# Sparse attention as four strands beside dense products, score tiles in accumulator banks, and a tile's wide products in a run

## The chip, the core and the metric

The kernel runs on one NeuronCore of a Trainium2 chip. TensorE (PE) multiplies into eight PSUM banks, VectorE (DVE) and ScalarE (ACT) empty those banks and do the elementwise work, GpSimd (POOL) does a little elementwise work in SBUF, and SyncE (SP) issues the loads. The metric is the device time of one execution in microseconds. Before the change the median of three runs is 1178.96 us (1177.51 to 1179.39).

## What is computed

Two transformer layers over 256 tokens of width 1024, everything in float32:

```python
for layer in range(DEPTH):                       # DEPTH = 2
    h = layer_norm(ALPHA * h + 0.5 * swiglu(h, ffn_w_in[layer, 0], ffn_w_out[layer, 0]), ...)
    mix = hybrid_mixer(h, ...) if layer % 2 == 0 else nsa_mixer(h, positions, ...)
    h = layer_norm(ALPHA * h + mix, ...)
    h = layer_norm(ALPHA * h + 0.5 * swiglu(h, ffn_w_in[layer, 1], ffn_w_out[layer, 1]), ...)

def swiglu(x, w_in, w_out):                      # inner width 2816
    gate, up = jnp.split(x @ w_in, 2, axis=-1)
    return (jax.nn.silu(gate) * up) @ w_out
```

So there are four feed-forward stages, one hybrid stage and one sparse attention stage (`nsa_mixer`). Sparse attention has 16 query heads in 2 groups of 8; a group shares its keys and values. For each block of 128 queries it adds three attentions, each weighted by a gate: over 15 compressed key blocks (a small two-layer network over 32 tokens each), over the selected blocks, and over a window. With 256 tokens there are four selectable blocks of 64 and up to eight may be taken, so the selected attention is causal attention over all keys, and the window of 512 also covers all of them. Both use keys turned by a partial rotary embedding. The sum over heads goes through an output product.

## The kernel before

Every product is made from float32 numbers that are split in two float32r parts, hi and lo: hi by hi, hi by lo and lo by hi are added up in one PSUM bank. `split` copies hi (ACT or DVE) and subtracts it (DVE) for lo. Weights arrive in `raw` tiles of 1 MB, of which there are three, and every weight part is split on the chip into `whi` and `wlo` tiles: one ACT or DVE copy, and one DVE subtraction (`wlo<-raw,whi`) each.

Nothing is issued as it is written. The class `Plan` records all operations of the program, and `Plan.order` lays them out with a list scheduler: each engine takes the ready operation that can start first, and among equals the one recorded earliest; its prices and buffer rules decide the order on each engine. On the chip every engine then runs its list strictly in that order. Within the stages the recording order is set by `weave`: it takes turns among generators (strands), each with a weight, so that the strand with the least PE work per weight is next; a strand that yields `'wait'` is passed over.

PSUM is dealt out by tag: `ps` has 2 banks, `mp` 2, `acc` 4. `ps` serves projections, `mp` transposes and small products, `acc` the sums of output products.

**Feed-forward stages.** Most inner features are made with weights as the stationary side: `proj_two` makes one tile of 128 features for all 256 tokens. Its stationary weights `whi` meet x's hi and lo parts side by side (one matmul of 512 columns), and `wlo` meets x's hi part (256 columns). Over the eight slices of the width it records them in turn, 512, 256, 512, 256. Each step of 256 features loads one `raw` tile for the gate and one for the up half and calls `proj_two` four times.

**The sparse attention stage** (`nsa`). `b` is the block of 128 queries or tokens (0 or 1), `g` the head group. `kv(b)` makes keys, values and gates of block b, `queries(g, w, bs)` makes queries (two transposes through `mp`, with the rotary turn between them), `keys(b)` turns the keys and splits them into `kd` hi and lo. `compress()` makes the compressed keys and values, `cmp_probs(b)` their probabilities, `attend(g, b)` the two other attentions with all of the output of a group and block, and `out_g0` the part of the output product that needs only group 0. In `attend` a score tile fills one bank: two heads of 128 keys for block 0, one head of 256 keys for block 1, each twice (selected and window). DVE takes the row maxima out of the bank (`TENSOR_REDUCE`), ACT the exponentials (`P`), then the tile is scaled (`P<-P,arena`, 128x1024, DVE or POOL), transposed through `mp` and copied (`PT`), and multiplied with the values (`vtok`).

Before the change these lines set the order of that stage:

```python
for b in range(2):
    kv(b)
    for _ in queries(0, wq, [b]):
        pass
    keys(b)
...
SB, turn = (("ps", "ps", "acc"), ("ps",)), [0]
...
self.weave([(attention(), W_NSA[0]), (rest(), W_NSA[1]), (out_g0(), W_NSA[2])])
```

So all keys and all queries of group 0 come first, then three strands: attention; `rest`, which is the first part of `compress`, the queries of group 1, the second part of `compress` and `cmp_probs`; and `out_g0`.

Of the kernel before, what the change touches and what calls it, by code (L numbers as in the profile page):

```python
# [13 lines left out]
OP = mybir.AluOpType  # L14
# [4 lines left out]
P = 128  # L19
# [20 lines left out]
NSA_ORDER = 1  # L40
W_HYB, W_OUT, W_NSA = (90.0, 94.0), (15.0, 21.0), (55.0, 45.0, 20.0)
# [477 lines left out]
class K:  # L519
# [201 lines left out]
    def proj_tok(self, x, b, w, ps):  # L721

        mm = self.nc.tensor.matmul
        for k in range(KD):
            xh, xl = self.xb(x, b, k)
            mm(ps, xh, w[k][0], start=k == 0, stop=False)
            mm(ps, xl, w[k][0], start=False, stop=False)
        for k in range(KD):
            mm(ps, self.xb(x, b, k)[0], w[k][1], start=False, stop=k == KD - 1)

# [734 lines left out]
    def nsa(self, x, then):  # L1465
# [6 lines left out]

        def chunk(r):
# [14 lines left out]
        def kv(b):  # L1488
            for r in range(2):
                ps = self.bank("ps")  # L1490
                self.proj_tok(x, b, ws[r], ps[:, :280])
# [3 lines left out]
        self.rope_tables()  # L1495
# [34 lines left out]
        def queries(g, w, bs):  # L1530
            gs = slice(g * 512, (g + 1) * 512)
            for b in bs:
# [17 lines left out]
                for e, (hi, lo) in enumerate(((up, dn), (dn, up))):  # L1550
                    src = H3(pt, 4)[hi]
                    self.copy(s[hi, :, e, :], src)
                    V.tensor_tensor(s[lo, :, e, :], src, s[hi, :, e, :].bitcast(F32), OP.subtract)
        kd = [self.m4(1024, f"kd{n}", dtype=F32R).rearrange("p (g r t) -> p g r t", g=2, r=2) for n in range(2)]
# [24 lines left out]
        state = dict(q=False, c=False, o=-1)  # L1579

        def compress():
            F = self.m4(1024, "F").rearrange("p (v g t) -> p v g t", v=2, g=2)
            pr = self.sm([32, P], "pr")
            with self.late():
                nc.sync.dma_start(pr, i['nsa_cmp_pos'][0].rearrange("v (i two) d -> (v i) (two d)", two=2))
            pt = self.bank("mp")
            nc.tensor.transpose(pt[:, :32], pr, self.ident[:32, :32])
            pos = self.sm([P, 2, 16], "cpos")
            V.tensor_copy(pos, H3(pt[:, :32], 2))
            w2r = self.sm([P, 2, 2, 64], "w2r")  # L1590
            with self.late():
                nc.sync.dma_start(w2r, i['nsa_cmp_w2'][0].rearrange("v (a p) d -> p v a d", p=P))
            w2d = self.sm([P, 2, 2, 64], "w2d")
            for c in range(2):
                nc.gpsimd.tensor_copy(w2d[:, :, c, :], w2r[:, 0])
            w = self.unit_cols(w_in, 1024, 256)
            X = self.m4(1024, "X").rearrange("p (v k g c) -> p v k g c", v=2, k=16, g=2)
            nc.gpsimd.memset(X[:, :, :, :, 15:16], 0.0)
            for v in range(2):
                ps = self.bank("ps")[:, :T]  # L1600
                yield from self.proj_steps(x, w[v], ps)
# [8 lines left out]
            yield 'mid'  # L1610
# [43 lines left out]
        def cmp_probs(b):  # L1654
# [19 lines left out]
            V.tensor_tensor(ev, ev, mx[:, 2, :, None].to_broadcast([P, 16, 15]), OP.mult)  # L1674
            yield
# [3 lines left out]
            self.copy(eT[b], H3(pt[:, :256], 2))  # L1679

# [6 lines left out]
        SB, turn = (("ps", "ps", "acc"), ("ps",)), [0]  # L1687

        def attend(g, b):
            N = (b + 1) * P  # L1690
            per = 2 - b
            gv = gat[:, b, :].rearrange("p (h r) -> p r h", r=3)
            PT = {}
            for half in range(2):
                sc = self.sm([P, 2, 2, 4], "asum", bufs=4)
                tiles = []
                for h0 in range(0, 4, per):
                    ps = self.bank(SB[g][turn[0] % len(SB[g])])
# [6 lines left out]
                    for n in range(per):  # L1705
                        h = half * 4 + h0 + n
# [18 lines left out]
                hs = g * 8 + half * 4  # L1725
# [170 lines left out]
```

## Time and profile before

| | |
|---|---|
| median of 3 runs | 1178.96 us |
| the profiled execution | 1176.69 us |
| its span, first to last instruction | 1175.0 us |
| mean granted TensorE clock | 0.98 of 2.4 GHz |
| PE, DVE, ACT, POOL busy | 1139.2, 897.6, 499.8, 47.9 us |
| sparse attention stage | 827.3 to 981.7 us of the span |

The profile comes from one execution. A line of the page or of an answer names engine, operation, the tile written, the tiles read, shapes and the number of instructions. PE's busy time counts matmuls whose ends are modelled and overlap, so the time from one matmul's start to the next one's is the better measure of its cost. The granted clock is 1.00 at 2.4 GHz and 0.50 at 1.2 GHz.

### The profile page before, as it was taken

How to read it: one execution, taken by the hardware profiler on the slowest of the kernel's cores; microseconds unless marked ns; L12 is line 12 of the kernel's file. 1: busy time of each engine (PE TensorE's matmuls, PEld its weight loads, DVE VectorE, ACT ScalarE, POOL GpSimd, SP SyncE). 2: the span in 40 equal slices, each digit the busy share in tenths (PEclk: the TensorE clock that was granted, in tenths of full speed). 3: DMA queues.
4: the chain of work that ended last, by engine and by line, in shares of the span. 5: the costliest groups of instructions: out<-in, count | busy, mean ns of one | idle time of the engine just before them, and what ended most of it. 6: DMA issues, size and time to landing. Idle time of an engine off the chain costs nothing.

```text
span 1175.0 us, 16522 instructions
## 1 busy us (share of the span) xinstructions
PE 1139.2 (97%) x6572; PEld 961.5 (82%) x6572; DVE 897.6 (76%) x1494; ACT 499.8 (43%) x911; POOL 47.9 (4%) x75
## 2 busy tenths in 40 slices
PE   8999999998999999999999999999998889999997
PEld 6888888898899777888888888888976667888886
DVE  7977778789699889777768967775867778777755
ACT  5534332367334555533333633333446345433320
POOL 1000000001021000000000000000002000000000
PEclk9999999999999999999999999999988799999999
DMA  8866553542305346755563756545236326755520
GB/s 298 310 188 200 194 201 90 161 155 95 108 30 188 121 164 217 251 181 179 193 203 119 272 180 204 186 150 183 86 99 147 105 72 215 251 198 180 192 75 36
DMA packets 144166, 196.14 MB, mean 167 GB/s; under 512 B 9277, under 2 KB 121050, under 8 KB 144090
## 3 DMA queue, kind: packets, MB, share of 16 engines
q1 hardware_dynamic: 144090, 195.10, 50.4%
q8 instruction: 51, 0.84, 0.3%
q14 instruction: 25, 0.20, 0.1%
HBM read 194.04 MB, written 1.05 MB: 166 GB/s over the span
## 4 chain that ended last, share of the span: by engine, by line
PE 88%; DVE 6%; DMA 2%; ACT 2%; issue 1%; SPq 0%; DVEq 0%; ACTq 0%
PE ps L495 53%; PE acc L495 29%; PE mp L495 6%; DVE wlo L495 2%; DMA raw<-in_ffn_w_in_dram 1%; DVE h L495 1%; DVE arena L495 1%; DMA raw<-in_nsa_w_out_dram 1%; DMA arena<-in_nsa_cmp_pos_dram 0%; SPq L495 0%; DVE x L495 0%; DVE cv L495 0%; ACT sw L495 0%; DVE lnst L495 0%; ACT P L495 0%
## 5 line engine op out<-in xcount | busy, mean ns | idle before, releaser
L495 PE MATMUL ps<-x,whi 128*128 128x512 f32 (+2 forms) x1680 | 516.9, 367 | 8.4 <-DVE cv L495 4.9
L495 DVE TENSOR_TENSOR wlo<-raw,whi 128x1024 fp32r<-128x1024 f32 (+1 forms) x349 | 415.7, 1212 | 9.8 <-ACT whi L495 6.5
L495 PE MATMUL ps<-x,wlo 128*128 128x256 f32 (+1 forms) x1432 | 404.7, 283 | 0.0
L495 PEld LDWEIGHTS ps<-x,whi 128*128 128x128 f32 (+1 forms) x1680 | 302.3, 190 | 64.4 <-issue 6.9
L495 PEld LDWEIGHTS ps<-x,wlo 128*128 128x128 f32 (+1 forms) x1432 | 272.1, 190 | 2.9
L495 ACT ACTIVATE whi<-raw 128x1024 fp32r<-128x1024 f32 (+1 forms) x243 | 245.5, 1049 | 24.9 <-DMA raw<-in_ffn_w_in_dram 17.0
L495 PE MATMUL acc<-whi,g 128*128 128x512 f32 x704 | 230.9, 391 | 0.0
L495 ACT ACTIVATE sg<-ps 128x256 f32<-128x256 f32 x162 | 62.2, 384 | 351.6 <-PE ps L495 351.4
L495 DVE TENSOR_TENSOR sg<-ps,sg 128x256 f32<-128x256 f32 x162 | 68.7, 424 | 165.1 <-ACT sg L495 165.0
L495 PEld LDWEIGHTS acc<-whi,g 128*128 128x128 f32 x704 | 132.2, 188 | 29.4
L495 PE MATMUL acc<-wlo,g 128*128 128x512 f32 x352 | 137.8, 392 | 0.0
L495 PE MATMUL ps<-whi,x 128*128 128x512 f32 (+1 forms) x480 | 126.5, 389 | 3.3 <-DVE whi L495 2.4
L495 PEld LDWEIGHTS ps<-whi,x 128*128 128x128 f32 x480 | 86.3, 190 | 23.0 <-DVE whi L495 3.7
L495 PEld LDWEIGHTS acc<-wlo,g 128*128 128x128 f32 x352 | 66.1, 188 | 10.9
L495 DVE CAST whi<-raw 128x1024 fp32r<-128x1024 f32 (+2 forms) x106 | 71.7, 678 | 4.1 <-DMA raw<-in_ffn_w_in_dram 2.9
L495 PE MATMUL ps<-wlo,x 128*128 128x512 f32 (+1 forms) x240 | 67.7, 382 | 0.0
L495 PE MATMUL acc<-whi,x 128*128 128x512 f32 x192 | 67.0, 413 | 0.1
L495 PEld LDWEIGHTS ps<-wlo,x 128*128 128x128 f32 x240 | 43.4, 189 | 7.7
L495 ACT ACTIVATE sg<-sg 128x256 f32<-128x256 f32 x74 | 31.1, 421 | 38.1 <-DVE sg L495 38.1
L495 POOL TENSOR_TENSOR lnve<-lnve,mhalf 128x1 f32<-128x1 f32 x12 | 11.4, 953 | 797.8 <-DVE lnve L495 797.8
L495 PEld LDWEIGHTS acc<-whi,x 128*128 128x128 f32 x192 | 35.7, 189 | 9.8 <-issue 2.8
L495 DVE SCALAR_TENSOR_TENSOR cv<-ps,arena,cv 128x255 f32<-128x255 f32 (+2 forms) x84 | 39.9, 477 | 4.8 <-ACT cv L495 3.8
(245 smaller groups left out, 971.9 us busy)
## 6 DMA issues: line engine op xcount, KB each, us to landing
raw<-in_ffn_w_in_dram SPq DMA_DIRECT2D x74, 1024.0 KB, 5.0
raw<-in_ffn_w_out_dram SPq DMA_DIRECT2D x44, 1024.0 KB, 5.0
raw<-in_hyb_w_in_dram SPq DMA_DIRECT2D x22, 1024.0 KB, 5.0
raw<-in_ffn_w_in_dram SPq DMA_DIRECT2D x26, 512.0 KB, 4.0
raw<-in_hyb_w_out_dram SPq DMA_DIRECT2D x8, 1024.0 KB, 4.8
raw<-in_nsa_w_in_dram SPq DMA_DIRECT2D x5, 1024.0 KB, 5.1
raw<-in_nsa_cmp_w_dram SPq DMA_DIRECT2D x4, 1024.0 KB, 5.7
raw<-in_nsa_w_out_dram SPq DMA_DIRECT2D x8, 512.0 KB, 7.7
```

The costliest lines, as they stand in the source:

```text
L495: r = getattr(getattr(nc, eng), fn)(*[res(a) for a in args], **{k: res(a) for k, a in kw.items()})
```

## The change

It has three parts.

1. `proj_two` records a tile's eight products of 512 columns first, and then its eight of 256.
2. The sparse attention stage is recorded as four strands with the weights 70, 55, 30 and 10: `attention`, `dense`, `compressed`, `out_g0`. `dense` is keys and values of block 0, queries of group 0 and block 0, keys and values of block 1, the first part of the compression (`compress_in`), queries of group 0 and block 1, and the queries of group 1. So attention of block 0 is recorded beside the products of block 1. Strands wait for what they need by names in a set `done`. The gate's sigmoid is done for each block by itself. The position table and the small second weights of the compression, and the tables of the rotary turn, are loaded and made at the stage's beginning.
3. Score tiles take their banks by `NSA_SB`: group 0, block 0 in `acc` alone, group 0, block 1 in `acc` and `ps` in turn, group 1 in `ps` alone. A tile's heads are now every other head of a group and not four neighbours, so the weights of the output product are loaded in plain rows: four loads of 1 MB on 128 partitions, where there were eight of 512 KB on 64 partitions.

```diff
-NSA_ORDER = 1
-W_HYB, W_OUT, W_NSA = (90.0, 94.0), (15.0, 21.0), (55.0, 45.0, 20.0)
+NSA_SB = (("acc",), ("acc", "ps"), ("ps",), ("ps",))
+W_HYB, W_OUT, W_NSA = (90.0, 94.0), (15.0, 21.0), (70.0, 55.0, 30.0, 10.0)
...
         for k in range(KD):
             mm(ps, w[0][:, k, :], x[2][:, k].rearrange("p h b t -> p (h b t)"), start=k == 0, stop=False)
+        for k in range(KD):
             mm(ps[:, :T], w[1][:, k, :], self.xk(x, k)[0], start=False, stop=k == KD - 1)
...
-        for b in range(2):
-            kv(b)
-            for _ in queries(0, wq, [b]):
-                pass
-            keys(b)
-        self.sigmoid(gat, gat)
-        for b in range(2):
-            self.scale_h(b)
+        def dense():
+            for b in range(2):
+                yield from kv(b)
+                if b == 1:
+                    yield from compress_in()
+                yield from queries(0, wq, [b])
+                keys(b)
+                self.sigmoid(gat[:, b], gat[:, b])
+                done.add(("k", b))
+                self.scale_h(b)
+                yield
+            yield from queries(1, self.tok_weights(w_in, 512, 512), range(2))
...
-                    ps = self.bank(SB[g][turn[0] % len(SB[g])])
+                    ps = self.bank(SB[2 * g + b][turn[0] % len(SB[2 * g + b])])
...
-                        h = half * 4 + h0 + n
+                        h = 2 * (h0 + n) + half
...
+                    yield from wait(("k", b), ("q", g, b))
                     yield from attend(g, b)
-                state['o'] = g
+                    done.add(("o", g, b))
-        def rest():
-            cmp = compress()
-            for r in cmp:
-                if r == 'mid' and NSA_ORDER:
-                    break
-                yield
-            yield from queries(1, self.tok_weights(w_in, 512, 512), range(2))
-            state['q'] = True
-            yield from cmp
+        def compressed():
+            yield from compress()
             for b in range(2):
+                yield from wait(("q", 0, b), ("q", 1, b))
                 yield from cmp_probs(b)
-            state['c'] = True
...
-            srcs = [(lambda r, s=s: v3(r)[HALF[s]], w_out[g, s, :, j0:j0 + 2, :]) for s in range(2)]
-            parts = self.unit(srcs, [lambda r, e=e: v3(r)[:, e, :] for e in range(2)])
+            parts = self.unit_rows(w_out, 2 * t, 2, 0, D)
...
-        self.weave([(attention(), W_NSA[0]), (rest(), W_NSA[1]), (out_g0(), W_NSA[2])])
+        self.weave(list(zip((attention(), dense(), compressed(), out_g0()), W_NSA)))
```

What this does to the engines' lists shows at three places. The first is PE in the last feed-forward stage, where `ps` is a tile of `proj_two`, `x` the stage's input and `sg` an earlier tile that is transposed. Before:

```order
L495 MATMUL ps_9152<-x_8884,whi_8924 128x512
L495 MATMUL ps_9152<-x_8884,wlo_8938 128x256
L495 MATMUL ps_9152<-x_8884,whi_8924 128x512
L495 MATMUL mp_9167<-ident_116,sg_9154 128x128 x2
L495 MATMUL ps_9152<-x_8884,wlo_8938 128x256
```

And after, the same tile and the next:

```order
L496 MATMUL ps_9151<-x_8895,whi_8911 128x512 x7
L496 MATMUL mp_9164<-ident_116,sg_9153 128x128 x2
L496 MATMUL ps_9151<-x_8895,whi_8911 128x512
L496 MATMUL ps_9151<-x_8895,wlo_8960 128x256 x8
L496 MATMUL ps_9184<-x_8895,whi_8950 128x512 x8
L496 MATMUL ps_9184<-x_8895,wlo_8992 128x256 x8
```

Wide and narrow products, which took turns, now stand in two runs of eight; the number of matmuls on PE is the same in the whole program (6097).

The second place is PE at the first scores. `whi` and `wlo` at 128x512 make queries, at 128x280 keys and values, `fixed` adds the causal mask, and `kd,qs` are scores. Before, they follow the queries of block 1, and take one bank of `ps` and one of `acc`:

```order
L495 MATMUL ps_7867<-wlo_7695,x_7621 128x512
L495 MATMUL ps_7867<-whi_7637,x_7621 128x512
L495 MATMUL ps_7917<-fixed_3920 128x512
L495 MATMUL ps_7917<-kd_1224_7818,qs_1223_7811 128x256
L495 MATMUL ps_7917<-kd_1226_7836,qs_1223_7811 128x256
L495 MATMUL ps_7917<-kd_1224_7818,qs_1223_7811 128x256
L495 MATMUL ps_7917<-kd_1226_7836,qs_1223_7811 128x256
L495 MATMUL acc_7645<-kd_1224_7818,qs_1223_7811 128x256
L495 MATMUL ps_7926<-x_7621,whi_7851 128x256
```

After:

```order
L496 MATMUL ps_7784<-wlo_7457,x_7625 128x280 x2
L496 MATMUL ps_7850<-whi_7474,x_7625 128x280 x4
L496 MATMUL acc_7649<-kd_1230_7845,qs_1228_7825 128x256
L496 MATMUL acc_7652<-kd_1230_7845,qs_1228_7825 128x256
L496 MATMUL acc_7778<-kd_1230_7845,qs_1228_7825 128x256
L496 MATMUL acc_7782<-kd_1230_7845,qs_1228_7825 128x256
L496 MATMUL ps_7850<-whi_7474,x_7625 128x280 x2
L496 MATMUL ps_7850<-whi_7507,x_7625 128x280
L496 MATMUL acc_7649<-kd_1233_7858,qs_1228_7825 128x256
```

All four score tiles of group 0 and block 0 now come in the middle of block 1's keys and values, in four `acc` banks at once, and `ps` is left to the projections.

The third place is DVE at the scores of group 0 and block 1 (`arena<-acc` or `<-ps`, 128x2, are the row maxima; `qs` and `kd` are splits of queries and keys, `q_` and `qT` belong to the making of the queries, and the `arena` of 128x64 is scratch of the rotary turn). Before:

```order
L495 COPY qT_1246_7937<-mp_8199 128x512
L495 TENSOR_REDUCE arena_8222<-ps_8189 128x2
L495 TENSOR_REDUCE arena_8222<-acc_8194 128x2
L495 CAST qs_1283_8233<-mp_8217 64x4x128
L495 TENSOR_REDUCE arena_8222<-ps_8207 128x2
L495 TENSOR_TENSOR qs_1283_8233<-mp_8217,qs_1283_8233 64x4x128 x2
L495 TENSOR_REDUCE arena_8222<-ps_8256 128x2
```

After:

```order
L496 TENSOR_TENSOR wlo_8211<-raw_8094,whi_8167 128x1024
L496 TENSOR_TENSOR wlo_8222<-raw_8094,whi_8169 128x1024
L496 TENSOR_TENSOR kd_1233_7858<-mp_8209,kd_1230_7845 128x4x128
L496 TENSOR_TENSOR arena_8155<-q_1220_7780,arena_3900 128x64
L496 TENSOR_TENSOR wlo_8250<-raw_8125,whi_8226 128x1024
L496 TENSOR_TENSOR q_1220_7780<-arena_8155 128x8x8 x2
L496 TENSOR_REDUCE arena_8269<-acc_8228 128x2
L496 TENSOR_REDUCE arena_8269<-ps_8239 128x2
```

Splits of the output product's weights, which used to follow the scores, now stand ahead of them in DVE's list.

## Rows read from the trace of the kernel before

**Rows 1.** The page's first section: busy us, share of the span, instructions.

```profile
PE 1139.2 (97%) x6572; PEld 961.5 (82%) x6572; DVE 897.6 (76%) x1494; ACT 499.8 (43%) x911; POOL 47.9 (4%) x75
```

**Rows 2.** Stretches: length, busy of PE, PEld, DVE, ACT, POOL, clock, DMA share, GB/s.

```profile
400.00:827.30 427.30, 426.60 (x2180) 357.17 (x2179) 327.23 (x505) 175.43 (x293) 7.96 (x7) 1.00 0.56 185
827.30:981.70 154.40, 138.79 (x811) 109.59 (x810) 114.69 (x205) 76.61 (x210) 13.87 (x19) 0.89 0.40 117
```

**Rows 3.** The same columns for five stretches of the sparse attention stage.

```profile
859.00:872.00 13.00, 10.16 (x54) 9.14 (x55) 9.88 (x20) 7.28 (x33) 0.53 (x2) 0.74 0.16 45
872.00:886.00 14.00, 14.00 (x63) 9.97 (x62) 4.87 (x11) 2.01 (x4) 0.60 (x2) 1.00 0.00 0
898.00:910.00 12.00, 9.34 (x69) 7.81 (x68) 9.68 (x15) 9.27 (x24) 3.42 (x2) 0.73 0.87 195
910.00:923.00 13.00, 9.12 (x51) 8.24 (x50) 11.78 (x25) 4.69 (x6) 1.25 (x1) 0.50 0.89 246
923.00:935.00 12.00, 12.00 (x74) 7.55 (x72) 6.17 (x11) 6.26 (x21) 0.00 (x0) 0.96 0.00 0
```

**Rows 4.** PE timeline, two tiles of `proj_two`: start us, us, what, count, idle before.

```profile
559.04 0.39 PE L495 MATMUL ps<-x,whi 128*128 128x512 f32 x1
559.27 0.28 PE L495 MATMUL ps<-x,wlo 128*128 128x256 f32 x1
...
564.68 0.40 PE L495 MATMUL acc<-whi,g 128*128 128x512 f32 x1
```

**Rows 5.** PE timeline where matmuls of 512 and of 256 columns stand in runs.

```profile
380.03 0.28 PE L495 MATMUL ps<-x,wlo 128*128 128x256 f32 x1
...
385.43 0.29 PE L495 MATMUL ps<-x,wlo 128*128 128x256 f32 x1
...
981.67 3.79 PE L495 MATMUL ps<-whi,x 128*128 128x512 f32 x16
985.29 1.98 PE L495 MATMUL ps<-wlo,x 128*128 128x512 f32 x8
```

**Rows 6.** The page's DMA issues: count, KB each, median us to landing.

```profile
raw<-in_ffn_w_in_dram SPq DMA_DIRECT2D x74, 1024.0 KB, 5.0
...
raw<-in_nsa_w_out_dram SPq DMA_DIRECT2D x8, 512.0 KB, 7.7
```

**Rows 7.** Pieces of the chain that ended last, within the attention stage: start, us.

```profile
855.93 5.66 DMA arena<-in_nsa_cmp_pos_dram
...
891.82 8.47 DMA raw<-in_nsa_w_out_dram
```

**Rows 8.** PE timeline: waits in the attention stage, idle us before and its releaser.

```profile
904.32 0.80 PE L495 MATMUL ps<-fixed 128*128 128x512 f32 x1 [1.55 <-ACT P L495]
...
964.75 2.16 PE L495 MATMUL mp<-ident,P 128*128 128x128 f32 x8 [3.22 <-DVE P L495]
```

**Rows 9.** DVE by form, 850 to 980 us: count, busy us, mean ns, idle before.

```profile
L495 DVE TENSOR_TENSOR wlo<-raw,whi 128x1024 fp32r<-128x1024 f32 x20 | 23.7, 1216 | 0.8 <-ACT whi L495 0.8
L495 DVE TENSOR_TENSOR P<-P,arena 128x1024 f32<-128x1024 f32 x8 | 10.8, 1361 | 0.1
L495 DVE TENSOR_REDUCE arena<-ps 128x2 f32<-128x512 f32 x13 | 8.8, 687 | 3.3 <-PE ps L495 3.1
...
L495 DVE TENSOR_TENSOR qs<-mp,qs 64x512 fp32r<-64x512 f32 x6 | 4.1, 689 | 0.8 <-ACT qs L495 0.7
```

**Rows 10.** DVE timeline: row maxima that follow one another.

```profile
888.23 0.68 DVE L495 TENSOR_REDUCE arena<-ps 128x2 f32<-128x512 f32 x1
888.83 0.68 DVE L495 TENSOR_REDUCE arena<-acc 128x2 f32<-128x512 f32 x1
```

**Rows 11.** PE timeline: narrow products of the attention stage.

```profile
829.80 1.19 PE L495 MATMUL ps<-wlo,x 128*128 128x280 f32 x8
830.83 2.10 PE L495 MATMUL ps<-whi,x 128*128 128x280 f32 x15
```

More of the change, by code (lines that the diff above doesn't have):

```diff
@@ L1470, in nsa @@
         BIG = 2.0 ** 100
+        pr = self.sm([32, P], "pr")
+        w2r = self.sm([P, 2, 2, 64], "w2r")
+        with self.late():
+            nc.sync.dma_start(pr, i['nsa_cmp_pos'][0].rearrange("v (i two) d -> (v i) (two d)", two=2))
+            nc.sync.dma_start(w2r, i['nsa_cmp_w2'][0].rearrange("v (a p) d -> p v a d", p=P))
+        pt = self.bank("mp")
+        nc.tensor.transpose(pt[:, :32], pr, self.ident[:32, :32])
+        pos = self.sm([P, 2, 16], "cpos")
+        V.tensor_copy(pos, H3(pt[:, :32], 2))
+        w2d = self.sm([P, 2, 2, 64], "w2d")
+        for c in range(2):
+            nc.gpsimd.tensor_copy(w2d[:, :, c, :], w2r[:, 0])
+        self.rope_tables()
         def chunk(r):
@@ L1553, in queries @@
                     V.tensor_tensor(s[lo, :, e, :], src, s[hi, :, e, :].bitcast(F32), OP.subtract)
+                done.add(("q", g, b))
         kd = [self.m4(1024, f"kd{n}", dtype=F32R).rearrange("p (g r t) -> p g r t", g=2, r=2) for n in range(2)]
@@ L1566, in nsa, with wait, compress_in @@
         wq = self.tok_weights(w_in, 0, 512)
-        for b in range(2):
-            kv(b)
-            for _ in queries(0, wq, [b]):
-                pass
-            keys(b)
-        self.sigmoid(gat, gat)
-        for b in range(2):
-            self.scale_h(b)
+        done = set()
+        def wait(*what):
+            while not done.issuperset(what):
+                yield 'wait'
+        def dense():
[8 more added lines that the diff above has]
+                self.scale_h(b)
+                yield
+            yield from queries(1, self.tok_weights(w_in, 512, 512), range(2))
         kcb = self.sm([P, 2, 2, 16], "kcb")
         vbd = self.m4(1024, "vbd").rearrange("p (g n d) -> p g n d", g=2, n=8)
[L1579 to L1597, printed above, removed]
+        F = self.m4(1024, "F").rearrange("p (v g t) -> p v g t", v=2, g=2)
+        X = self.m4(1024, "X").rearrange("p (v k g c) -> p v k g c", v=2, k=16, g=2)
+        def compress_in():
+            wc = self.unit_cols(w_in, 1024, 256)
             nc.gpsimd.memset(X[:, :, :, :, 15:16], 0.0)
@@ L1609, in compress @@
                                     pos[:, v, a * 8:(a + 1) * 8, None, None].to_broadcast([P, 8, 2, 15]), OP.add)
-            yield 'mid'
+            done.add("X")
+        def compress():
+            yield from wait("X")
             for v in range(2):
@@ L1674, in cmp_probs @@
             V.tensor_tensor(ev, ev, mx[:, 2, :, None].to_broadcast([P, 16, 15]), OP.mult)
+            done.add(("e", b))
             yield
@@ L1679, in cmp_probs @@
             self.copy(eT[b], H3(pt[:, :256], 2))
+            done.add(("c", b))
         eT = [self.sm([P, 2, P], f"eT{b}") for b in range(2)]
@@ L1756, in attend @@
                     first = False
-            while not state['c']:
-                yield 'wait'
+            yield from wait(("c", b))
             yield
```

29 lines of the change are left out of this document (13 added, 16 removed).

## The prediction, made before the changed kernel was run

> **What bounds the kernel now.** I read the share of each engine first, then the windows by stage, then the stage that the change rewrites in smaller windows, then timelines. PE is busy for 97% of the span, DVE for 76% [rows 1]. In the feed-forward stretch PE is busy 426.6 of 427.3 us at granted clock 1.00 (2.4 GHz), DVE 327.2 of them (77%) [rows 2]: there PE alone sets the time, and what it saves arrives at the end until DVE's 100 us of slack are used up. The sparse attention stage is another case: of 154.4 us PE is idle for 15.6, and the mean clock is 0.89 [rows 2]. A mean of 0.89 between levels 1.00 and 0.50 is 22% of the stage, 34 us, at 1.2 GHz; work there takes twice its time, so up to 17 us are lost to the clock. Idle and clock together are 32.6 us, the most that any order of the same work can win: a floor of 121.8 us. If I instead add up each matmul's start-to-start time (below) PE's own work is 114.7 us, and DVE's busy time in the stage is by chance 114.7 too. So both engines have about three quarters of the stage to do; what matters is whether they do it at the same time.
>
> They do not. Where PE makes products (872 to 886, 923 to 935) it is busy without a break at a clock of 0.96 to 1.00 and DVE has 4.87 us of work in 14, and 6.17 in 12; where attention runs (910 to 923) DVE is busy 11.78 of 13 us, PE 9.12 at clock 0.50 [rows 3]. In 859 to 872 and 898 to 910 PE idles 2.84 and 2.66 us at a clock of 0.74 and 0.73. Over those three stretches idle time is 9.4 us, and time at half clock 6.8 + 6.5 + 13 = 26 us. Two pieces of the chain are DMAs: 5.66 us for the position table, 8.47 us for the output product's weights [rows 7].
>
> **The change, part one: wide and narrow products in runs.** Two alternating tiles take 564.68 - 559.04 = 5.64 us with 32 matmuls back to back: 2.82 us a tile, 352 ns for a pair of 512 and 256 columns [rows 4]. In runs a matmul of 512 costs (985.29 - 981.67) / 16 = 226 ns, and one of 256 (385.43 - 380.03) / 45 = 120 ns (45 matmuls start in between) [rows 5]. A tile in two runs: 8 x 0.226 + 8 x 0.120 = 2.77 us, 0.05 less. 74 loads of feed-forward weights [rows 6] feed two tiles each, 148 tiles: 148 x 0.05 = 7 us; the two changes of width that are left in a tile and the places where transposes already broke the turns take a little, so I count -6.5 us. The narrow run of rows 5 takes its stationary side from x, not from weights; so the ends are 0 (the alternation costs nothing of its own) and -8. Nothing is moved between engines, except that a tile needs `wlo` eight matmuls later, which can only help.
>
> The trace shows 352 ns for a pair against 346 in runs. The Trainium skill, page "TensorE: Matmul & The Clock Gate", section "Back-to-back issue gap", gives the isolated gap of a warm matmul as N/2.4 + 2.5 ns, by its own width alone. By that a tile is an estimated 8 x (215.8 + 109.2) ns = 2.60 us in either order, and the regrouping is worth nothing. The rows are above that figure in both orders and differ between them, which speaks for a price of changing width; the rule's result stands as a rival below.
>
> **Part two: the four strands.** PE's instructions in the stage are the same kinds and numbers. Priced by start-to-start time, 232 of 512 columns at 0.227, 96 of 280 at 1.03 / 8 = 0.129 [rows 11], 96 of 256 at 0.120 and the narrower rest at their own in this trace, they make the 114.7. I divide the changed stage at the first score tile of group 0 and block 1.
>
> *First half.* PE's own work there is 52.6 us: 87 x 0.227 + 65 x 0.120 + 96 x 0.129 = 39.9, and 12.7 of transposes and narrow products. It holds block 1's keys, values and compression products, and in their middle the scores of block 0. Four score tiles at once leave DVE four row maxima (0.687), two copies, a `wlo` (1.216) and small work, about 5.9 us [rows 9], while PE has 3.3 us left before it needs one of their results: a wait of 2.6. Like waits stand before the P tiles are transposed (1.361 for a scaling) and at `kd`. I take 5 us for them together: the same three kinds that cost 1.55 and 3.22 now [rows 8]. 57.6 us.
>
> *Second half.* PE has 62.1 us of work. DVE's list from the first row maximum of block 1 to the last split of the output holds 98 instructions, by the mean durations of rows 9 62.4 us; as two row maxima of 0.68 start 0.60 apart [rows 10], I take 0.08 off each: 54.6. DVE never was fuller than 11.78 / 13 = 0.91 [rows 3], so 60 us, with 1.2 of backlog at the start and 5.3 us that PE still has behind DVE's last split, 66.5. Late in this half the queries of group 1 are used up and only scores in two `ps` banks are left, each of which waits for a row maximum and an exponential; six tiles with about 0.6 of wait each are 3.5 us more. 70 us, with ends 62 (PE alone) and 78.
>
> *Clock.* PE would idle some 13 us of 127.6, in many short pieces and not in one stretch of 13 us as now. What the engine did before its clock fell was to idle a fifth or more of a stretch [rows 3]. I expect a third of today's 34 us at half clock, 12 us, which costs 6. Ends: 0 and 17.
>
> The stage: 57.6 + 70 + 6 = 133.6 against 154.4, **-21 us** (from -32.6, the floor, to -4, if waits and clock are as now save for the two loads).
>
> **What is free, and what covers it.** The position table is loaded at the stage's start, with some 25 us of products ahead of its use: the chain's 5.66 us vanish into those. Eight `w_out` loads at a median of 7.7 us become four of 1 MB; loads of 1 MB land in 5.0 [rows 6]. The gate's sigmoid in two halves adds three small DVE instructions, some 0.6 us, to the first half, where DVE has room (4.87 of 14 [rows 3]). Rotary products go to POOL, 4% busy [rows 1]. On SP's list the four compression loads now stand ahead of group 1's query weights and of `w_out`; with three `raw` tiles, each load waits for the matmuls of the load three before. That, and DVE's `wlo` splits of `w_out` which now stand ahead of group 0, block 1's row maxima (1.216 each [rows 9]), are the places where a new wait can arise. At the stage's end the last split, and in the next stage the first load, are as before.
>
> **The sum.** -6.5 - 21 = -27.5. The profiled execution took 1176.69, so 1149.2; the median of the runs lies 2.3 above it, so **1151.5, about 1152 us**.
>
> **Rivals.**
> - *The floor is reached.* PE stays fed, the clock falls nowhere, the stage is 122 us: 1179 - 6.5 - 32.4 = 1140 us. For it: nothing in the dense stretches kept PE waiting. Against it: DVE's 0.91 in any attention stretch. 0.12.
> - *The width change is free*, so part one gives nothing: 1179 - 21 = 1158 us. For it: only 2% separate the rows, from two different kinds of stationary side. Against it: both orders keep PE without a break, so the 6 ns a pair have no other source in these rows. 0.10.
> - *The waits return at the banks.* `ps` alone carries group 1's scores, where today it also does; with queries, keys and values done early there is nothing to put beside them, the clock is at 0.50 there for as long as in 910 to 923, and the stage wins only the two DMA pieces in part: -4 there, 1179 - 4 - 6.5 = 1168 us. 0.15.
> - *Slower: the load ring.* SP issues in order, and a load waits for the matmuls of the third before it. The compression weights' matmuls need X, and X comes from DVE's list behind block 0's row maxima. If the four loads behind them land only when asked for, each is exposed by its 5.0 us, 20 us, and the clock falls on top as in 898 to 910 (0.73, 3.2 us of 12, some 10 over four). 1179 - 27 + 30 = 1182 us. It decides if three or more of the four are fully exposed and at half clock. Against it: 0.40 of DMA is used in the stage [rows 2], and DVE has room when X is made. 0.06.
>
> **How the numbers follow.** The forecast (1145 to 1163) has 0.57, and the rivals have 0.12, 0.10, 0.15 and 0.06. The range leaves out the slower case and the edges of the floor and of the banks: 1140 to 1170. About 0.2% is what a measurement of this kernel can tell from no change. Only the ring crosses it upward (0.06); a time within 0.2% would need nearly all gains to be cancelled, 0.02; faster 0.92.
>
> **What will show it.** In the changed profile a tile of `proj_two` is about 2.77 us, with starts 226 and 120 ns apart (2.82 would say that the change of width is free). The sparse stage is near 134 us with a clock above 0.93, PE idle about 13 us and DVE's busy share near 0.85. In the first half PE waits on DVE for row maxima, on no position table. Were a `raw` load the releaser of PE's long waits, the ring rival holds; were it `ps` banks at a clock of 0.50, the banks. The prediction is most easily wrong in the second half: its 70 us rest on a DVE list that I priced, not saw.

## The result, and the profile after

The changed kernel takes 1152.94 us (median of four runs, 1150.78 to 1153.03), the kernel before 1178.63: a ratio of 0.978 with a 95% interval of 0.976 to 0.980, 25.7 us less. 1152 was predicted, and the range was 1140 to 1170. The profiled execution has a span of 1151.0 us where the kernel before had 1175.0, so the trace shows 24.0 us of it.

The first section of the page (busy us, share of the span, instructions), of the changed kernel, answers to [rows 1]:

```profile
PE 1122.2 (97%) x6572; PEld 952.2 (83%) x6572; DVE 890.2 (77%) x1488; ACT 500.1 (43%) x910; POOL 54.1 (5%) x84
```

PE has the same 6572 instructions and 17.0 us less busy time. Where that was, the windows show: length, busy time of PE, PEld, DVE, ACT and POOL with instructions, granted clock, DMA share, GB/s. The rows are the feed-forward stretch, the two halves of the sparse stage as the prediction divided it (at the first score product of group 0 and block 1), and the whole stage.

```profile
396.00:823.50 427.50, 426.79 (x2198) 360.02 (x2198) 328.02 (x508) 176.30 (x292) 8.68 (x9) 1.00 0.58 187
823.50:881.50 58.00, 54.78 (x384) 45.24 (x383) 41.58 (x85) 25.91 (x72) 6.09 (x14) 1.00 0.48 159
881.50:959.00 77.50, 72.14 (x427) 53.30 (x426) 65.76 (x113) 48.80 (x137) 13.17 (x13) 0.98 0.33 107
823.50:959.00 135.50, 126.93 (x810) 98.54 (x809) 107.34 (x197) 74.71 (x208) 19.26 (x26) 0.99 0.40 129
```

Beside [rows 2]: the sparse stage went from 154.4 to 135.5 us. PE's idle time in it fell from 15.6 to 135.50 - 126.93 = 8.6, and its busy time from 138.8 to 126.9 at a clock of 0.99 instead of 0.89. That is 18.9 of the 24.0 us. The other 5.1 lie outside the stage, where the products now stand in runs. In the feed-forward stretch a span of almost the same length holds 18 more matmuls (2198 for 2180).

Four smaller windows of the stage answer to [rows 3]:

```profile
883.00:895.00 12.00, 10.10 (x57) 8.23 (x56) 11.87 (x23) 8.81 (x29) 0.53 (x4) 1.00 0.25 87
895.00:907.00 12.00, 9.89 (x61) 7.87 (x62) 8.48 (x22) 8.46 (x34) 6.70 (x5) 0.86 0.29 90
...
919.00:931.00 12.00, 12.00 (x74) 8.46 (x75) 10.07 (x20) 8.40 (x26) 2.85 (x1) 1.00 0.24 74
...
943.00:959.00 16.00, 15.25 (x90) 10.26 (x88) 15.94 (x23) 11.95 (x16) 0.99 (x1) 1.00 0.59 189
```

What one is to see: where PE is busy without a break (919 to 931), DVE now has 10.07 us of work in 12, not 6.17 in 12; and nowhere does the clock stand at 0.50 for 13 us. Only 895 to 907, where PE idles 2.1 of 12 us, shows 0.86. At the stage's end DVE is the full engine: 15.94 of 16. Over the whole stage DVE is busy for 107.34 / 135.50 = 0.79, not the 0.85 that was forecast.

PE's waits in the first half of the stage (us in total, times, longest), and in the second:

```profile
PE ps L496 <- DVE wlo L496: 1.5, 1, 1.5
PE mp L496 <- DVE arena L496: 1.0, 1, 1.0
...
```

```profile
PE ps L496 <- ACT P L496: 2.7, 3, 1.1
PE acc L496 <- DVE kd L496: 0.7, 1, 0.7
PE acc L496 <- ACT x L496: 0.7, 1, 0.7
...
```

No wait is longer than 1.5 us, where [rows 8] had 3.22, and none is put down to a DMA. The chain of work that ended last (start, us, what) still has a DMA in it, where the kernel before had two [rows 7]:

```profile
859.95 8.55 DMA raw<-in_nsa_w_in_dram
...
868.52 0.70 DVE whi L496
```

That is a load of group 1's query weights behind the compression's. DVE's copy of it stands ahead of small work of the compression, for which PE then waits 1.0 us (the second line of the waits).

### The profile page after: what moved, and what is told of

Its sections match the earlier page's. It is cut to its first block, busy times and chain, and to the rows that moved or that the text cites. A ratio compares the mean times of both kernels' runs of the same rounds, so it can differ in the third digit from the quotient of the medians.

```text
span 1151.0 us, 16518 instructions
## 1 busy us (share of the span) xinstructions
PE 1122.2 (97%) x6572; PEld 952.2 (83%) x6572; DVE 890.2 (77%) x1488; ACT 500.1 (43%) x910; POOL 54.1 (5%) x84
## 4 chain that ended last, share of the span: by engine, by line
PE 87%; DVE 8%; ACT 2%; DMA 2%; issue 1%; SPq 0%; DVEq 0%; ACTq 0%
PE ps L496 53%; PE acc L496 28%; PE mp L496 5%; DVE wlo L496 3%; DVE arena L496 1%; DMA raw<-in_ffn_w_in_dram 1%; DVE h L496 1%; DMA raw<-in_nsa_w_in_dram 1%; DVE qs L496 1%; DVE x L496 1%; ACT P L496 1%; DVE cv L496 0%; DVE whi L496 0%; DVE lnst L496 0%; SPq L496 0%
## 5 line engine op out<-in xcount | busy, mean ns | idle before, releaser
L496 PE MATMUL ps<-x,whi 128*128 128x512 f32 (+2 forms) x1680 | 388.9, 361 | 6.6 <-DVE cv L496 4.9
L496 PEld LDWEIGHTS ps<-x,whi 128*128 128x128 f32 (+1 forms) x1680 | 296.3, 190 | 50.2 <-issue 6.2
L496 PE MATMUL ps<-x,wlo 128*128 128x256 f32 (+1 forms) x1432 | 237.1, 284 | 1.5 <-DVE wlo L496 1.5
L496 PEld LDWEIGHTS ps<-x,wlo 128*128 128x128 f32 (+1 forms) x1432 | 209.6, 191 | 13.6 <-DVE wlo L496 1.7
L496 DVE CAST whi<-raw 128x1024 fp32r<-128x1024 f32 (+1 forms) x105 | 71.1, 678 | 6.7 <-DMA raw<-in_ffn_w_in_dram 3.4
```

The costliest lines, as they stand in the source:

```text
L496: r = getattr(getattr(nc, eng), fn)(*[res(a) for a in args], **{k: res(a) for k, a in kw.items()})
```

## The experiments

Each kernel was timed against the kernel before on one chip. A difference to the changed kernel is taken from the two ratios. Where the stage's length is compared, it is that of the profiled execution, up to the first product of the last feed-forward stage. The first feed-forward stage, which no experiment on the sparse stage means to change, ended between 206.8 and 209.2 us in these traces, so some 2 us of a span belong to the start and to no edit. Engines' lists are laid out anew by the planner for each kernel, except for the last two, which keep the changed kernel's lists.

### The two parts apart

`e1_run_only`, the kernel before with the one edit:

```diff
             mm(ps, w[0][:, k, :], x[2][:, k].rearrange("p h b t -> p (h b t)"), start=k == 0, stop=False)
+        for k in range(KD):
             mm(ps[:, :T], w[1][:, k, :], self.xk(x, k)[0], start=False, stop=k == KD - 1)
```

> The kernel before with only the products of a tile in two runs. Theory: each change of width between neighbouring products costs a few ns, so 148 tiles lose 15 changes each. By the changed kernel's trace the feed-forward stages in sum are about 5.2 us shorter, so 1178.6 - 5.2 = 1173.4 us, within 1 us, and a tile takes about 2.78 us where it took 2.82. Rival (a product costs by its own width alone): no change, 1178.6 us, and the 5.2 us belong to something else.

Measured: 1171.6 us against 1178.9, ratio 0.994 (0.993 to 0.996), 6.8 us less.

`e2_strands_only`, the changed kernel without that line:

> The changed kernel with the wide and narrow products of a tile taking turns as before. Theory: the two parts lie in different stages and add up, so 1152.9 + 5.2 = 1158 us, within 1.5 us, with the sparse attention stage at about 135 us and a clock of 0.98 or more there. Rival (the parts help each other, for example because the stage starts with weights loaded earlier): more than 2 us away from 1158 us.

Measured: 1159.4 us, ratio 0.984 (0.983 to 0.986), 18.9 us less; its sparse stage takes 137.1 us at a clock of 0.96, where about 135 and 0.98 or more were expected. The product of both ratios, 0.994 x 0.984 = 0.978, is that of the whole change. The parts add up.

### What the alternation costs

`e3_run_of_two`, the kernel before, with the products of a tile two by two:

```diff
-        for k in range(KD):
-            mm(ps, w[0][:, k, :], x[2][:, k]..., start=k == 0, stop=False)
-            mm(ps[:, :T], w[1][:, k, :], self.xk(x, k)[0], start=False, stop=k == KD - 1)
+        for k0 in range(0, KD, 2):
+            for k in range(k0, k0 + 2):
+                mm(ps, w[0][:, k, :], x[2][:, k]..., start=k == 0, stop=False)
+            for k in range(k0, k0 + 2):
+                mm(ps[:, :T], w[1][:, k, :], self.xk(x, k)[0], start=False, stop=k == KD - 1)
```

> The kernel before with two products of 512 columns and then two of 256, four times a tile: half as many changes of width as in the kernel before. Theory (a price for each change): about half of what the full run gains, -2.6 us, 1176.0 us. Rival one (what costs is a 512-column product between two of 256 columns, which pairs already avoid): nearly the full gain, 1173.5 to 1174.5 us. Rival two (only long runs are cheaper): 1178.6 us.

Measured: 1169.8 us, ratio 0.993 (0.992 to 0.995), 8.0 us less (6.1 to 9.8): as much as the full run gives, not half. The theory that each change of width has its price falls. PE's timeline of two tiles, first of the changed kernel, then of this one (start, us, what, count):

```profile
490.77 1.98 PE L496 MATMUL ps<-x,whi 128*128 128x512 f32 x8
492.58 1.11 PE L496 MATMUL ps<-x,wlo 128*128 128x256 f32 x8
493.53 2.00 PE L496 MATMUL ps<-x,whi 128*128 128x512 f32 x8
495.38 1.12 PE L496 MATMUL ps<-x,wlo 128*128 128x256 f32 x8
496.33 0.40 PE L496 MATMUL acc<-whi,g 128*128 128x512 f32 x1
```

```profile
489.61 0.61 PE L495 MATMUL ps<-x,whi 128*128 128x512 f32 x2
490.06 0.40 PE L495 MATMUL ps<-x,wlo 128*128 128x256 f32 x2
490.30 0.63 PE L495 MATMUL ps<-x,whi 128*128 128x512 f32 x2
490.76 0.39 PE L495 MATMUL ps<-x,wlo 128*128 128x256 f32 x2
...
495.17 0.40 PE L495 MATMUL acc<-whi,g 128*128 128x512 f32 x1
```

Both take 5.56 us (496.33 - 490.77, 495.17 - 489.61), the alternating tiles 5.64 [rows 4]. Over the 144 undisturbed tiles of each trace the mean is 2.819 us alternating, 2.782 in pairs and 2.780 in runs. The median times from a product's start to the next one's start say where. A product of 512 columns takes 236 ns between two of 256 and 233 in pairs; in a run of eight the first, behind a narrow one, takes 233 and all others 227, also the last, which a narrow one follows. One of 256 takes 117 between two of 512, 115 and 119 in pairs, and in a run 113 for the first and 120 for the others. So a narrow product beside wide ones is not the dear one; a wide product between two narrow ones is.

### Strands and banks

`e5_scores_after_dense` takes back what the change is named after:

```diff
-                    yield from wait(("k", b), ("q", g, b))
+                    yield from wait(("k", 1), ("q", 0, 1), ("q", g, b))
                     yield from attend(g, b)
```

> The changed kernel, but attention of block 0 starts only when keys and group 0's queries of both blocks are done, as in the kernel before; four strands, banks, loads and runs stay. Theory (the gain of the stage is that VectorE and ScalarE work on block 0 while TensorE makes block 1's products): the row maxima, exponentials, scalings and copies of group 0 and block 0 fall into the part of the stage where DVE is the busy one, about 10 us of DVE work, and TensorE idles there and its clock falls in part: 8 to 15 us longer, 1161 to 1168 us. Rival (the gain comes from the banks, the earlier loads and the compression products that were moved forward): within 2 us, 1152 to 1155 us.

Measured: 1158.2 us, ratio 0.983 (0.981 to 0.984), 5.5 us more than the changed kernel. In its windows (first half, second half, the whole stage, the last feed-forward stage) one sees where:

```profile
824.80:879.40 54.60, 53.03 (x375) 44.61 (x374) 39.94 (x75) 26.39 (x73) 7.16 (x20) 1.00 0.49 169
879.40:963.00 83.60, 76.24 (x437) 53.27 (x435) 69.22 (x117) 46.52 (x133) 11.05 (x15) 0.98 0.33 104
824.80:963.00 138.20, 129.27 (x810) 97.88 (x808) 109.16 (x190) 72.91 (x205) 18.22 (x34) 0.99 0.39 130
963.00:1155.70 192.70, 184.64 (x952) 157.37 (x952) 134.44 (x210) 67.61 (x113) 2.84 (x3) 0.99 0.47 159
```

The first half is 3.4 us shorter and the second 6.1 longer; the stage is 2.7 us longer, and the last stage takes 192.7 instead of 192.0 (the span is 4.7 us longer; 1.3 lie ahead of the stage). Neither theory holds: the 8 to 15 us did not come, and the effect is not nothing. That block 0's attention stands in the middle of block 1's products is worth some 2.7 us in the stage, and perhaps less, for the planner also laid out the end of the stage in another way. PE's timeline there (start, us, what, count, idle before), first of the changed kernel, then of this one:

```profile
957.42 0.60 PE L496 MATMUL mp<-ident,h 128*128 128x128 f32 x4
...
958.78 0.39 PE L496 MATMUL acc<-whi,x 128*128 128x512 f32 x1
959.01 3.80 PE L496 MATMUL ps<-whi,x 128*128 128x512 f32 x16
```

```profile
960.81 0.39 PE L496 MATMUL acc<-whi,x 128*128 128x512 f32 x1
961.28 1.29 PE L496 MATMUL mp<-ident,h 128*128 128x128 f32 x8
963.04 0.73 PE L496 MATMUL ps<-whi,x 128*128 128x512 f32 x2 [0.48 <-DVE x L496]
964.24 3.72 PE L496 MATMUL ps<-whi,x 128*128 128x512 f32 x15 [0.46 <-DVE x L496]
```

In the changed kernel the transposes of the stage's result (`mp<-ident,h`) stand between the last output products, here behind them, with waits of 0.48 and 0.46 us for the next stage's input. How much of the 2.7 us that is, no run separates.

`e4_old_banks`:

```diff
-NSA_SB = (("acc",), ("acc", "ps"), ("ps",), ("ps",))
+NSA_SB = (("ps", "ps", "acc"), ("ps", "ps", "acc"), ("ps",), ("ps",))
```

> The changed kernel with score tiles in the banks that they had before: group 0 takes ps, ps, acc in turn, group 1 ps alone. Theory banks (block 0's four score tiles at once in acc, so that ps stays free for the projections, is what keeps TensorE fed): the stage gets 4 to 12 us longer, 1157 to 1165 us, with waits of ps tiles for exponentials as the largest waits of PE. Theory strands (where the work stands counts, not the bank): within 2 us of the changed kernel, 1151 to 1155 us.

Measured: 1165.3 us, ratio 0.990 (0.988 to 0.991), 13.9 us more than the changed kernel by the ratios. The windows (the whole stage, then three pieces of it) and four rows of PE's timeline with its waits:

```profile
822.30:968.90 146.60, 136.08 (x811) 104.00 (x810) 109.28 (x199) 75.38 (x205) 18.78 (x27) 0.93 0.37 122
```

```profile
835.00:847.00 12.00, 7.84 (x35) 5.71 (x33) 6.72 (x17) 4.58 (x20) 1.35 (x5) 0.77 0.01 1
847.00:859.00 12.00, 12.00 (x63) 9.43 (x63) 8.15 (x13) 5.29 (x23) 0.00 (x0) 0.80 0.00 0
...
895.00:907.00 12.00, 7.86 (x25) 5.42 (x24) 11.24 (x24) 9.39 (x34) 1.30 (x4) 0.69 0.42 135
```

```profile
836.48 0.50 PE L496 MATMUL ps<-fixed 128*128 128x512 f32 x1 [0.46 <-ACT q L496]
...
845.76 0.79 PE L496 MATMUL ps<-fixed 128*128 128x512 f32 x1 [1.04 <-ACT P L496]
...
847.21 3.12 PE L496 MATMUL ps<-whi,x 128*128 128x280 f32 x12
...
898.37 0.73 PE L496 MATMUL ps<-kd,qs 128*128 128x512 f32 x2 [1.93 <-ACT P L496]
```

The mask products of two score tiles (`ps<-fixed`, at 835.63 and 836.48 us) take both `ps` banks before the queries and keys are ready. The projections of block 1 have no bank until exponentials have emptied one, and start at 847.21. Until then PE has little to put beside the making of queries and keys: it is busy 7.84 of 12 us, and of its 4.2 idle us only 1.04 are put down to an exponential, the others to the queries and keys (ACT, POOL, DVE). Its clock falls to 0.77, and the next stretch is at 0.80 although PE is then busy all the time. In the changed kernel the masks go to `acc`, and block 1's projections follow right behind them:

```profile
837.08 0.62 PE L496 MATMUL acc<-fixed 128*128 128x512 f32 x2
837.53 0.68 PE L496 MATMUL ps<-whi,x 128*128 128x280 f32 x4
```

That is the wait which the `acc` banks avoid. The third piece is the same for block 1's scores: a score tile waits 1.93 us for an exponential. As in `e5_scores_after_dense` the transposes of the stage's result stand behind its last product here.

`e9_three_strands` goes back to the three strands, with everything else of the change kept (banks, runs, early loads, order of heads):

```diff
-                if b == 1:
-                    yield from compress_in()
...
-            yield from queries(1, self.tok_weights(w_in, 512, 512), range(2))
...
         def compressed():
+            yield from compress_in()
+            yield from queries(1, self.tok_weights(w_in, 512, 512), range(2))
             yield from compress()
...
-        self.weave(list(zip((attention(), dense(), compressed(), out_g0()), W_NSA)))
+        for _ in dense():
+            pass
+        self.weave([(attention(), 55.0), (compressed(), 45.0), (out_g0(), 20.0)])
```

> The changed kernel with the strands of the kernel before: keys, values and queries of group 0 of both blocks first, then attention, the rest (first part of the compression, queries of group 1, second part of the compression) and the output product with weights 55, 45, 20; runs, banks, early loads, the split sigmoid and the order of heads stay. Theory strands (the order of dense work and compression, above all the compression weights' loads ahead of group 1's queries, keeps TensorE fed and its clock up): the stage loses 10 to 18 us of its 18.6, 1163 to 1171 us, with a mean clock there near 0.90. Rival (banks, early loads and order of heads carry the gain): 1153 to 1158 us.

Measured: 1166.2 us, ratio 0.990 (0.988 to 0.991), 14.0 us more. The stage's window and PE's two largest waits:

```profile
823.00:972.10 149.10, 136.59 (x810) 105.91 (x809) 118.00 (x209) 75.75 (x208) 10.25 (x18) 0.91 0.36 120
```

```profile
PE mp L496 <- DVE arena L496: 4.3, 1, 4.3
PE mp L496 <- DVE P L496: 4.1, 2, 3.8
```

The first wait ends with the transposes of the compressed attention's probabilities, which DVE makes; in the changed kernel all waits of that kind come to 1.0 us. The four strands make the compression earlier: its weights' products end at 867 us, in the kernel before at 900 and in this one at 894. That this order is what removes the waits fits a comparison with `e5_scores_after_dense`: there block 0's attention also starts only behind the keys and queries of both blocks, but the four strands stay and the compression's products end at 860, and the stage takes 138.2 us, not 149.1. So 2.7 us at most belong to block 0's attention among block 1's products, and some 11 to the place of the compression and of group 1's queries, with the strands' weights; these were not taken apart further.

`e10_three_strands_old_banks` joins the edits of the last two:

> As e9_three_strands, and the old banks too, so that only the runs, the early loads, the split sigmoid and the order of heads of the change are left. If strands and banks are all of the stage's gain: as the kernel with runs alone, 1170 to 1173 us. If loads and the order of heads bring part of it: below 1168 us. Compared with e9_three_strands it says what the banks are worth without the strands: theory 0 to 3 us.

Measured: 1167.8 us, ratio 0.991 (0.990 to 0.993), 15.7 us more. So without the strands the banks are worth 1 to 2 us, with them 14; the strands without the banks about as little (both within the intervals of the ratios). Most of the stage's gain is there only with both. The time at half clock within the stage goes the same way: 34.1 us in the kernel before, 27.3 in this one and in `e9_three_strands`, 20.5 in `e4_old_banks`, and 3.4 in the changed kernel. About 4 us lie between this kernel and the one with runs alone: loads, sigmoid and heads, in that order of the work.

### What the prediction counted as free

`e7_late_position` loads and prepares the position table and the small second weights at the beginning of `compress_in` again:

> The changed kernel, but the position table and the small second weights are loaded and prepared with the compression's first products and no longer at the stage's beginning. The prediction counted the 5.66 us piece of the chain of the kernel before as hidden by the early load. If the early load is what hides it: 2 to 5 us longer, 1155 to 1158 us, with PE or DVE waiting for that load. If the compression has other cover now: within 1 us, 1152 to 1154 us.

Measured: 1157.2 us, ratio 0.982 (0.981 to 0.983), 4.8 us more. Its windows (the stage, the last feed-forward stage):

```profile
824.80:962.90 138.10, 128.75 (x810) 98.74 (x808) 111.29 (x203) 72.29 (x200) 17.43 (x25) 0.98 0.39 130
962.90:1155.80 192.90, 184.82 (x952) 157.21 (x952) 134.46 (x210) 68.35 (x113) 2.84 (x3) 0.99 0.47 158
```

The stage is 2.6 us longer and the last stage 0.9. No wait of PE or DVE in it is put down to the position table's load. The time is there, the mechanism that I named is not shown: here too the transposes of the stage's result stand behind its last product, as in `e5_scores_after_dense`, and I did not separate the two.

`e8_old_heads` puts back four neighbouring heads in a tile and the eight loads on 64 partitions:

```diff
-                        h = 2 * (h0 + n) + half
+                        h = half * 4 + h0 + n
...
-            parts = self.unit_rows(w_out, 2 * t, 2, 0, D)
+            srcs = [(lambda r, s=s: v3(r)[HALF[s]], w_out[g, s, :, j0:j0 + 2, :]) for s in range(2)]
+            parts = self.unit(srcs, [lambda r, e=e: v3(r)[:, e, :] for e in range(2)])
```

> The changed kernel with a tile's heads four neighbours again, and the output product's weights in eight loads of 512 KB on 64 partitions. The prediction counted this part at nothing. Theory (the loads stand well ahead of their use now): within 1.5 us of the changed kernel, 1151.5 to 1154.5 us, though a load takes longer (7.7 us in the kernel before, 5.0 in the changed). Rival (the 8.47 us piece of the chain of the kernel before was that form of load, and it returns): 2 to 6 us longer.

Measured: 1154.4 us, beside 1154.3 of the changed kernel in the same session. The load takes 7.8 us at the median instead of 5.0, and no wait of PE is put down to it. The stage takes 137.2 us in this profile, beside 135.7 in that of the changed kernel in the same session, which the times do not show. This part was free, and gives nothing that can be told from noise.

### What sets the pace of the stage

Two kernels keep every engine's list as it is in the changed kernel and repeat DVE instructions in place; `e13_changed_again` is the changed kernel in that session.

```diff
+        if op[1] == "tensor_reduce" and op[3].get("negate"):
+            twice.append(op)
```

> The changed kernel with each of the 24 row maxima of the score tiles done twice in a row, everything else in the same place: 24 x 0.60 = 14.4 us more on DVE, 20 of the 24 in the second half of the stage. Theory of the prediction (the second half is set by DVE's list and by the chain from score to maximum to exponential): 9 to 15 us longer, 1162 to 1168 us, and the clock of the second half falls below 0.95. Rival (PE sets the pace, and DVE's 11.7 idle us of the second half take it up): 0 to 4 us.

```diff
+        if op[0] == "vector" and op[1] == "tensor_tensor" and op[2][1].t in plan.w_out:
+            twice.append(op)
```

> The changed kernel with each of the eight subtractions that split the output product's weights done twice in a row, everything else in the same place: 8 x 1.13 = 9 us more on DVE, in no chain of scores. Theory (DVE's list as a whole sets the second half): 5 to 9 us longer, 1158 to 1162 us. Rival (only DVE work between a score and its exponential counts): 0 to 3 us, while the run with the maxima doubled gets at least twice as much per us added.

> The changed kernel itself, in the same session as the kernels below, so that they have a time beside them from the same chip: 1152.9 us, within 2 us. In its trace the sparse attention stage should again take 135 to 136 us at a clock of 0.98 or more; the first feed-forward stage may differ by some 2 us, as it did among the kernels so far (its end lay between 206.8 and 209.2 us).

Measured: 1154.3 us for the changed kernel; 1169.9 with the maxima twice, 15.6 more for 14.4 us of added work; 1162.5 with the weights' subtractions twice, 8.2 more for 9.0. The second halves of the two:

```profile
886.50:976.10 89.60, 78.08 (x428) 55.79 (x427) 78.91 (x133) 49.66 (x137) 12.66 (x13) 0.90 0.28 92
```

```profile
881.90:969.40 87.50, 78.44 (x428) 58.36 (x427) 75.20 (x121) 49.20 (x137) 14.89 (x13) 0.90 0.30 94
```

DVE is busy 0.88 and 0.86 of it, in the changed kernel 65.76 / 77.50 = 0.85. Its idle time is not used up by more work: 10.7, 12.3 and, in the changed kernel, 11.7 us. The second halves are 12.1 us longer for 13.2 us more of DVE's busy time, and 10.0 for 9.4: a microsecond more on DVE is about a microsecond more of this half, in the chain of scores or not. The rival, that PE sets the pace and DVE's idle time takes up the work, falls. But DVE does not set it alone. Its idle time in the changed kernel's second half is waiting for others; the two largest lines (us, times, longest) are

```profile
DVE PT L496 <- PE mp L496: 2.8, 5, 1.5
DVE arena L496 <- ACT P L496: 2.1, 3, 0.9
```

and of the 11.0 us that the profile lists, 8.2 are for PE (transposes and scores) and 2.8 for ACT. What sets the pace is DVE's list with these handovers; no run adds work on PE or ACT.

The stage in all these kernels (length and busy time from the windows over the whole stage, PE idle as their difference):

| kernel | stage us | PE idle | PE busy | clock | DVE busy |
|---|---|---|---|---|---|
| before | 154.4 | 15.6 | 138.8 | 0.89 | 114.7 |
| three strands, old banks | 152.1 | 15.4 | 136.7 | 0.91 | 115.7 |
| three strands | 149.1 | 12.5 | 136.6 | 0.91 | 118.0 |
| old banks | 146.6 | 10.5 | 136.1 | 0.93 | 109.3 |
| scores after dense | 138.2 | 8.9 | 129.3 | 0.99 | 109.2 |
| changed | 135.5 | 8.6 | 126.9 | 0.99 | 107.3 |
| changed again | 135.7 | 7.4 | 128.3 | 0.97 | 107.5 |

## Why the prediction was right, step by step

**The sum.** -27.5 us were forecast, -6.5 outside the sparse stage and -21 in it. Measured are -25.7; in the traces -5.1 outside and -18.9 in the stage, which takes 135.5 us where 133.6 were forecast.

**The bound.** Right. In the feed-forward stages PE's saving arrived whole. The sparse stage was two engines in turn, and now they work at once. The prediction did not price the parts of that apart: block 0's attention among block 1's products brings 2.7 us of the stage at most, and the place of the compression and of group 1's queries, together with the banks, the rest.

**Part one, -6.5 us.** Right in size: 6.8 by the ratio (5.1 to 8.6), 148 x 0.039 = 5.8 by the tiles' means. The reason I gave, a price of changing width, fell with pairs, which have half of the changes and the whole gain. The Trainium skill, page "TensorE: Matmul & The Clock Gate", section "Back-to-back issue gap", gives the isolated gap of a matmul by its own width alone, so that the order would be worth nothing and a pair would take an estimated 325 ns. The traces do not agree: they show 352 ns for an alternating pair and 348 in runs. What in TensorE makes a wide product between two narrow ones dear stays open.

**First half of the stage.** 57.6 us forecast, 58.0 measured. The waits are there, 3.2 us in the profile where 5 were forecast, but the longest, 1.5 us, is for a `wlo`, which the prediction had among the 5.9 us of DVE work and not as the one that ends last.

**Second half.** 70 us and most of 6 for the clock were forecast, 77.5 measured: right in sum and wrong in its split. That the two errors nearly cancel, 7.5 us too little for DVE's list and its surroundings and most of 6 too much for the clock, is luck. The stretch from the first row maximum to the last split of the output:

```profile
885.20:953.30 68.10, 63.51 (x384) 46.49 (x382) 56.39 (x100) 40.43 (x127) 11.18 (x9) 0.97 0.30 96
```

The DVE list was right (100 instructions and 56.4 us, 98 and 54.6 forecast). Its share was not: I took 0.91 from a window of 13 us in which DVE had work heaped up; over 68 us it is 56.39 / 68.10 = 0.83. That makes 68.1 where the prediction had 60 and 3.5 for the banks. The tail behind it, 959.0 - 953.3 = 5.7 us, was forecast as 5.3, and the start, 885.2 - 881.5 = 3.7, as 1.2.

**Clock.** Mis-sized: 12 us at half clock were expected. The changed kernel has 3.4 (896.4 to 899.8 us), which cost at most 1.7; the prediction's twice the time at half clock is a bound, for a product of 256 columns takes 213 ns from start to start at 0.50 in the kernel before, and 120 at 1.00. The clock is also less of a cause than I took it for. In the second profile of the same kernel it is 0.97, with 6.8 us at half (896.4 to 903.2), and the stage is 0.2 us longer: where DVE sets the pace, a slower PE only waits less (7.4 us idle instead of 8.6). How much of the 11.9 us of lost PE busy time was the clock's own in the kernel before, and how much would have been waiting otherwise, no run separates.

**PE's own work.** By the 114.7 us of the prediction, which I did not measure again, PE would be without work of its own for 135.5 - 114.7 = 20.8 us, where 13 and 6 for the clock were forecast. The profile shows 8.6 of them as idle; the other 12.2 lie in what it counts as busy, up to 1.7 of them the clock. That the rest is short waits under the modelled ends of matmuls is likely and not shown. Of the waits that the profile lists in the stage, 4.5 us are for DVE and 4.0 for ACT.

**What was free.** The heads and the loads of the output weights: right, 0. The early position table: its load has vanished from the chain, as forecast; 4.8 us are lost when it goes back, and how much of that is the load's is not shown. For the added sigmoid no run was made alone.

**The rivals.** The floor was not reached. The load ring came at one place of the four, the 8.55 us load above, and cost PE 1.0 us of waiting there and not 5 to 8: other products were ready to cover it. The banks were rightly feared, but they are the price of leaving the change half done (`e4_old_banks`, 1165.3 us; 1168 was the rival's time).

## What to carry to other kernels

When two engines take turns, ask for each stretch which of them has work left that could stand there, and check that the buffers between them allow it: here the new order without the new banks, and the banks without the order, each lost three fifths to three quarters of the stage's gain (146.6 and 149.1 us, between 154.4 and 135.5). A busy share that is taken from a full window of a dozen us is not what an engine keeps up over a whole stage with chains between engines; take it from the longest stretch that has the same kind of work. And test the pace by repeating an instruction in place with the lists held: that showed that DVE's work lengthens this stage one for one. Where stages are compared, let every window end at the same instruction: here the last transposes stand before the last product in one kernel and behind it in another, and a window that ends with that product hides 2 us.

## What the runs showed of the hardware that I had not expected

A matmul's start-to-start time depends on what stands around it: 227 ns for 512 columns in a run behind another wide product, 233 behind a narrow one or in pairs, 236 between two narrow ones; and a narrow product behind a wide one is quicker (113 to 117 ns) than in a run (120). And the granted clock can be lower while the stage hardly gets longer, as in the second run of the changed kernel (0.97 and 135.7 us beside 0.99 and 135.5), so a low clock beside waits is no proof that the clock is what costs.
